# Splitting the key-score weights early: 34 weight tiles split during the second block's attention and kept split in DRAM

## The chip, the cores and the metric

One core of one Trainium2 chip runs the kernel. Times are device microseconds (us) of one execution, from a profile or from timed runs; lower is better. The kernel's own clock starts at its first instruction ("span"); a timed run also holds what lies around the span.

## The reference, cut to what matters

The program is two transformer blocks over 512 tokens of width 1024, float32. Only the second half of the second block matters here: attention with a merge of two branches, and then `peer`, a product-key lookup over a table of 16384 experts.

```python
def peer(h, wq, keys1, keys2, u_tab, v_tab):        # cut
    q = (xc @ wq).reshape(chunk, 8, 2, 128)
    s1, s2 = q[:, :, 0] @ keys1, q[:, :, 1] @ keys2  # 128 scores each, per head
    v1, i1 = top_k(s1, 16); v2, i2 = top_k(s2, 16)
    best, pos = top_k(all 256 sums v1 + v2, 16)      # 16 experts per token and head
    g = softmax(best)
    a = u_tab[eidx] . xc                             # first table
    return (gelu(a) * g) . v_tab[eidx]               # second table
```

## The kernel before, in words

Every float32 product is made of three fp32r products (`mm3`, lines 87 to 89): both operands are split into a high part, `hi`, and a low part, `lo = src - hi`. `split` (lines 66 to 70) makes `hi` with one copy on ACT (L69) and `lo` with one subtraction on DVE (L70), or on POOL where `eng=nc.gpsimd` is given. `wload` (lines 72 to 85) loads a weight tile of 128x1024 floats (512 KB) through the SP queue into one of 4 raw buffers `wraw`, and splits it into one of 3 buffers `whi` and one of 3 buffers `wlo`. These three pools serve the whole kernel.

The order on each engine is made when the kernel is built, by a list scheduler that simulates the program: among the instructions that are ready it takes the one that stands first in the program. In `peer` the order on POOL, and late in it on DVE, is that of the program text. A generator class `Fill` (lines 33 to 44) lets one piece of the program hand out its steps inside the loops of another.

The stages around the change, all in order:

- **Attention of the second block** (`block2`, 8 heads). Each turn of the loop over `h` makes half of a merge tile (`half_merge`: a `w2g` tile and half a `w2b` tile), in every second turn also the next queries (`q_prep`), then the weighted values of head `h` (`values`: transposes, split of the transposed probabilities, products) and the scores of the next head.
- **Merge** (L1370 to L1381): 8 turns over `m`, each with a `w2g` tile, half a `w2b` tile and a few sums.
- **Output projection and norm**: start of `peer`, with 8 `w2o` tiles.
- **Score stage** (`peer`, L1523 to L1602): for each of 8 heads, `scores(h)` loads two tiles of the queries' weights `pwq` (L1529, split with POOL), makes the queries and their 2x128 scores, and finds the top 16 of each on DVE (`top16`, L1388 to L1393); `best16(h)` adds the pairs on POOL (`cand`, L1551), takes the top 16 of the sums and turns them into expert numbers (L1562 to L1593, DVE and ACT). Between them stand `ahead(n)` calls: each runs one `u_chunk`, that is, one of 128 chunks of the first table, `puT[c]`, against all tokens of three tiles, with a gelu on ACT (L1430) and a store to `ad`. Chunks 0 to 27 are made here (4 before the stage's own loop, 2 in each `scores`, 1 in every second `best16`, 4 at the end), and their `lo` is made on POOL. POOL also gathers two table rows per head (L1493) and multiplies them (L1503) for the fourth token tile.
- **Table stages**: one-hot matrices with chunks 28 to 79, then the second table with chunks 80 to 127. Their chunks are split with DVE.

Of the kernel before, what the change touches and what calls it, by code (L numbers as in the profile page):

```python
# [9 lines left out]
F32 = mybir.dt.float32  # L10
F32R = mybir.dt.float32r
# [11 lines left out]
KD = D // 128  # L23
# [5 lines left out]
def f32(ap):  # L29
    return ap.bitcast(F32)  # L30
# [16 lines left out]
class Emit:  # L47
# [1010 lines left out]
            yield from self.filters(pool, psum)  # L1058


    def block2(self, es0):
        self.rstep = RSTEP
        tc, nc, A = self.tc, self.nc, self.A
        mm = nc.tensor.matmul
        tt, ts, stt = nc.vector.tensor_tensor, nc.vector.tensor_scalar, nc.vector.scalar_tensor_tensor
        with ExitStack() as es:
# [162 lines left out]
                            self.split(yhl[:, 0, j], yhl[:, 1, j], y)  # L1229

            pc = es.enter_context(tc.tile_pool(name="b2c", bufs=1))
            ohl = pc.tile([128, 2, 4, S], F32R, name="atT")
            mb = pc.tile([128, KD, S], F32, name="mb")
            with ExitStack() as e2:
# [115 lines left out]
                for h in range(8):  # L1350
                    cur = nxt
                    if h % 2 == 0 and h < 6:
                        nq.append(q_prep(h // 2 + 1))
                    if h < 7:
                        half_merge(1, h + 1, None)
                    values(h, *cur)
                    if h < 7:
                        nxt = scores(h + 1)
# [4 lines left out]
            with ExitStack() as e2:  # L1363
                self.banks(e2, 6)
                m2 = e2.enter_context(tc.tile_pool(name="mg22", bufs=2))
                mh = mg.tile([128, KD, S], F32R, name="mh2")
                ml = mg.tile([128, KD, S], F32R, name="ml2")
                g1 = mg.tile([128, D], F32, name="g1")
                self.dma(g1, self.mod[0:1, 2 * D:3 * D].to_broadcast([128, D]))
                for m in range(KD):  # L1370
                    ps = lin(A["w2g"][2 * m])
                    s = m2.tile([128, S], F32, name="sga")
                    nc.scalar.activation(s, ps, AF.Sigmoid)
                    wh, wl = self.wload(A["w2b"][m, :, 0:512])
                    ps = self.bank()
                    for k in range(4):
                        c = slice(k * 128, k * 128 + 128)
                        self.mm3(ps, wh[:, c], wl[:, c], ohl[:, 0, k], ohl[:, 1, k], k == 0, k == 3)
                    tt(s, ps, s, op=ALU.mult)
                    tt(s, s, mb[:, m], op=ALU.add)  # L1380
                    self.split(mh[:, m], ml[:, m], s)  # L1381
                self.merged = mh, ml, g1, mg


# [10 lines left out]
    def peer(self):  # L1395
# [9 lines left out]
        with ExitStack() as es:  # L1405
# [15 lines left out]
            b = self.mod_cols(pp, self.mod, 3 * D, "pb")  # L1421
            def u_chunk(c, eng=None):

                wh, wl = self.wload(A["puT"][c], eng=eng)
                p = self.acc()
                for k in range(KD):
                    s_ = slice(k * 128, k * 128 + 128)
                    self.mm3(p[:, :TD], wh[:, s_], wl[:, s_], hh[:, k, :TD], hl[:, k, :TD], k == 0, k == KD - 1)
                g = dn.tile([128, TD], F32, name="ga", bufs=4)
                nc.scalar.activation(g, p[:, :TD], AF.Gelu_apprx_tanh)  # L1430
                if c < AHEAD:
                    self.dma(ad[c], g)
                    return None
                return g
# [79 lines left out]
            with ExitStack() as ek:  # L1514
# [7 lines left out]
                def scores(h):  # L1522
                    val = pk.tile([128, NT, 2, 16], F32, name="tkv", bufs=3)  # L1523
                    ixu = pk.tile([128, NT, 2, 16], U32, name="tki", bufs=3)
                    keys = pk.tile([128, 256], F32, name="keys")
                    self.dma(keys, A["pkeys"][h])
                    for half in range(2):
                        wh, wl = self.wload(A["pwq"][2 * h + half], eng=nc.gpsimd if h >= 0 else None)
                        ps = self.acc()  # L1529
                        for k in range(KD):  # L1530
                            c = slice(k * 128, k * 128 + 128)
                            self.mm3(ps, wh[:, c], wl[:, c], hh[:, k], hl[:, k], k == 0, k == KD - 1)
                        q = pk.tile([128, S], F32, name="pq")
                        nc.scalar.activation(q, ps, AF.Copy)
                        p3 = self.bank()
                        for t in range(NT):
                            c = slice(t * 128, t * 128 + 128)
                            mm(p3[:, c], lhsT=q[:, c], rhs=keys[:, half * 128:half * 128 + 128], start=True, stop=True)
                        sk = pk.tile([128, NT, 128], F32, name="sk")
                        nc.scalar.activation(sk, p3.rearrange("p (t n) -> p t n", t=NT), AF.Copy)  # L1540
                        for t in range(NT):
                            self.top16(pk, sk[:, t], 128, val[:, t, half], ixu[:, t, half])
                        ahead(1)
                    return val, ixu
# [215 lines left out]

BLOCKS = ((0, 0, 2, 16), (32, 2, 2, 8), (48, 4, 4, 4), (64, 8, 8, 2))
GLAST = 122
GPOOL = 16
GSHARE = 0.34
OVERFLOW = True
# [172 lines left out]
```

## Time and profile before

| | us |
|---|---|
| median of 3 runs | 2734.28 (2725.38 to 2735.51) |
| the profiled execution, whole | 2726.15 |
| its span | 2724.4 |

One execution was profiled. PE is TensorE's matmuls, PEld its weight loads, DVE VectorE, ACT ScalarE, POOL GpSimd, SP the queue that issues most DMAs. A row of a view by line has: line, engine, operation, tile written <- tiles read, count, then busy time and mean duration, then the idle time of the engine just before and what ended it. "Busy" of an instruction runs from its start to its end, so an instruction that is held up after it started is counted as busy.

### The profile page before, as it was taken

What the parts mean: (1) busy time and instruction counts of PE and PEld (TensorE: products, weight loads), DVE (VectorE), ACT (ScalarE), POOL (GpSimd) and SP (SyncE); (2) the same over time, 40 slices, a digit from 0 to 9 for tenths busy, and PEclk for the clock granted to TensorE, in tenths of its full rate; (3) what the DMA queues carried; (4) which work ended last, traced back from release to release, by engine and by line L of the source; (5) the groups of instructions that cost most, each with busy time, mean ns of one, the idle gap of its engine ahead of it and who ended that gap; (6) DMA issues with size and microseconds to landing.
All of it is one profiled execution on the core that took longest, in us unless ns stands there. A gap on an engine that the chain in (4) does not pass through costs nothing. (4 is left out here: it accounts for less than half of the span.)

```text
span 2724.4 us, 33367 instructions
## 1 busy us (share of the span) xinstructions
PE 2451.1 (90%) x11725; PEld 1919.5 (70%) x11725; DVE 1853.3 (68%) x3133; ACT 1074.9 (39%) x1608; POOL 941.6 (35%) x777
## 2 busy tenths in 40 slices
PE   7999897879977979999798888999899999999997
PEld 5776566423335766668597778989688878988886
DVE  6677965334356576654649999988677767777676
ACT  4554434212215336653433435434433333333333
POOL 1002640101100320000145665430666665666661
PEclk9999998889988988999899889999699999999999
DMA  4115684789975211104543348997589998888884
GB/s 142 62 54 170 224 289 160 283 331 390 400 276 207 93 59 47 39 32 156 172 124 127 126 135 278 344 370 254 203 292 302 304 302 265 306 303 287 293 294 158
DMA packets 215934, 589.47 MB, mean 216 GB/s; under 512 B 30565, under 2 KB 85349, under 8 KB 214740
## 3 DMA queue, kind: packets, MB, share of 16 engines
q1 hardware_dynamic: 170836, 433.91, 45.8%
q0 software_dynamic: 44928, 153.42, 16.3%
q8 instruction: 92, 1.51, 0.2%
q14 instruction: 78, 0.64, 0.1%
HBM read 541.85 MB, written 53.78 MB: 219 GB/s over the span
## 5 line engine op out<-in xcount | busy, mean ns | idle before, releaser
L69 ACT ACTIVATE whi<-wraw 128x1024 fp32r<-128x1024 f32 (+1 forms) x290 | 299.8, 1035 | 489.8 <-PE acc L88 175.0
L87 PE MATMUL acc<-hph,whi 128*128 128x384 f32 (+1 forms) x1152 | 407.1, 354 | 30.1 <-ACT ga L1430 29.2
L89 PE MATMUL acc<-hph,wlo 128*128 128x384 f32 (+1 forms) x1152 | 404.1, 351 | 7.9 <-DVE wlo L70 7.3
L88 PE MATMUL acc<-hpl,whi 128*128 128x384 f32 (+1 forms) x1152 | 402.7, 350 | 0.0
L70 DVE TENSOR_TENSOR wlo<-wraw,whi 128x1024 fp32r<-128x1024 f32 (+1 forms) x242 | 296.8, 1227 | 140.0 <-ACT whi L69 138.0
L70 POOL TENSOR_TENSOR wlo<-wraw,whi 128x1024 fp32r<-128x1024 f32 x48 | 120.1, 2507 | 468.1 <-ACT whi L69 463.4
L87 PEld LDWEIGHTS acc<-hph,whi 128*128 128x128 f32 x1152 | 222.6, 193 | 42.3 <-ACT ga L1430 33.9
L87 PE MATMUL yp<-vhi,wah 128*128 128x512 f32 x732 | 228.4, 392 | 11.3 <-ACT wah L69 11.3
L89 PEld LDWEIGHTS acc<-hph,wlo 128*128 128x128 f32 x1152 | 221.6, 192 | 22.2 <-DVE wlo L70 14.8
L88 PE MATMUL yp<-vlo,wah 128*128 128x512 f32 x732 | 228.3, 391 | 0.0
L1676 POOL TENSOR_TENSOR gw<-gw,ga 128x256 f32<-128x256 f32 x128 | 179.6, 1403 | 141.0 <-DMA ga<-ad 78.0
L88 PEld LDWEIGHTS acc<-hpl,whi 128*128 128x128 f32 x1152 | 222.4, 193 | 7.3 <-DVE hpl L70 0.2
L89 PE MATMUL yp<-vhi,wal 128*128 128x512 f32 x732 | 225.1, 390 | 0.0
L70 DVE TENSOR_TENSOR vlo<-wraw,vhi 128x1024 fp32r<-128x1024 f32 x122 | 156.4, 1282 | 97.0 <-ACT vhi L69 96.9
L1493 POOL DMA_INDIRECT grow<-pu,ei x128 | 148.9, 1164 | 208.0 <-DVE grow L1506 169.5
L1493 POOL DMA_INDIRECT grow<-pvr,ei x128 | 172.6, 1349 | 113.4 <-DVE gy L1510 87.9
L69 ACT ACTIVATE wah<-gw 128x384 fp32r<-128x384 f32 x126 | 66.1, 524 | 276.9 <-POOL gw L1677 217.9
L1510 DVE SCALAR_TENSOR_TENSOR gy<-grow,wt,gy 128x1024 f32<-128x1024 f32 x127 | 164.0, 1291 | 11.5 <-DMA grow<-pvr,ei 9.3
L87 PEld LDWEIGHTS yp<-vhi,wah 128*128 128x128 f32 x732 | 138.0, 189 | 40.8 <-ACT wah L69 14.0
L70 DVE TENSOR_TENSOR wal<-gw,wah 128x384 fp32r<-128x384 f32 x126 | 93.9, 745 | 100.3 <-ACT wah L69 98.4
L89 PEld LDWEIGHTS yp<-vhi,wal 128*128 128x128 f32 x732 | 137.5, 188 | 30.3 <-DVE wal L70 1.8
L88 PEld LDWEIGHTS yp<-vlo,wah 128*128 128x128 f32 x732 | 138.2, 189 | 27.0
(669 smaller groups left out, 5168.8 us busy)
## 6 DMA issues: line engine op xcount, KB each, us to landing
wraw<-wgu SPq DMA_DIRECT2D x128, 512.0 KB
wraw<-puT SPq DMA_DIRECT2D x128, 512.0 KB
wraw<-pv SPq DMA_DIRECT2D x128, 512.0 KB
wraw<-wd SPq DMA_DIRECT2D x64, 512.0 KB
aw<-wada SPq DMA_DIRECT2D x48, 512.0 KB
gd<-gs SPq DMA_DIRECT2D x8, 2048.0 KB
gw<-gd SPq DMA_DIRECT2D x128, 128.0 KB
ad<-ga SPq DMA_DIRECT2D x80, 192.0 KB
```

Source lines behind the costliest of these rows:

```text
L69: nc.scalar.activation(hi, src, AF.Copy)
L70: (eng or nc.vector).tensor_tensor(lo, src, f32(hi), op=ALU.subtract)
L87: mm(ps, lhsT=wh, rhs=xh, start=first, stop=False)
L88: mm(ps, lhsT=wh, rhs=xl, start=False, stop=False)
L89: mm(ps, lhsT=wl, rhs=xh, start=False, stop=last)
L1493: nc.gpsimd.indirect_dma_start(out=r, out_offset=None, in_=A["pu" if i < 128 else "pvr"], in_offset=bass.IndirectOffsetOnAxis(ap=ei[:, s:s ...
L1510: stt(gy, r, wt[:, s:s + 1], gy, op0=ALU.mult, op1=ALU.add)
L1676: nc.gpsimd.tensor_tensor(gw[:, :TG], gw[:, :TG], g[:, :TG], op=ALU.mult)
```

## The change

A generator `presplit` hands out 34 steps: 16 tiles of `pwq` and the first 18 chunks of `puT`. A step loads the tile, splits it (copy on ACT, subtraction on POOL) and stores both halves to DRAM from POOL's queue. Three steps are handed out in each turn of the attention loop (24 in all) and two in each turn of the merge until none is left (the other 10, in five turns). In the score stage the 34 tiles are no longer split: their two halves are loaded straight into a `whi` and a `wlo` buffer.

```diff
+    def presplit(self):
+        tc, nc, A = self.tc, self.nc, self.A
+        self.qd = tc.dram_tile([16, 2, 128, 1024], F32, name="qd")
+        self.ud = tc.dram_tile([NPRE, 2, 128, 1024], F32, name="ud")
+        todo = [(A["puT"][i], self.ud[i]) for i in range(4)] + [(A["pwq"][i], self.qd[i]) for i in range(4)]
+        for i in range(4, max(16, NPRE)):
+            todo += [(A["pwq"][i], self.qd[i])] if i < 16 else []
+            todo += [(A["puT"][i], self.ud[i])] if i < NPRE else []
+        for src, dst in todo:
+            h, l = self.wload(src, eng=nc.gpsimd)
+            self.store(dst[0], f32(h))
+            self.store(dst[1], f32(l))
+            yield
+
+    def presplit_load(self, src):
+        hi = self.whi.tile([128, 1024], F32R, name="whi")
+        lo = self.wlo.tile([128, 1024], F32R, name="wlo")
+        self.dma(f32(hi), src[0])
+        self.dma(f32(lo), src[1])
+        return hi, lo
...
+            fill = Fill(self.presplit())
...
+                    fill(PFILL)
                     values(h, *cur)
...
                     self.split(mh[:, m], ml[:, m], s)
+                    fill(2 if m < KD - 1 else None)
...
-                wh, wl = self.wload(A["puT"][c], eng=eng)
+                wh, wl = self.presplit_load(self.ud[c]) if c < NPRE else self.wload(A["puT"][c], eng=eng)
...
-                        wh, wl = self.wload(A["pwq"][2 * h + half], eng=nc.gpsimd if h >= 0 else None)
+                        wh, wl = self.presplit_load(self.qd[2 * h + half])
...
+NPRE = 18
+PFILL = 3
```

## Rows read from the trace of the kernel before

**Rows 1.** The page's shares of the whole span
```profile
PE 2451.1 (90%) x11725; PEld 1919.5 (70%) x11725; DVE 1853.3 (68%) x3133; ACT 1074.9 (39%) x1608; POOL 941.6 (35%) x777
```

**Rows 2.** Busy time by stretch: attention, merge, projection, score stage
```profile
core 0: us, PE busy (x) PEld busy (x) DVE busy (x) ACT busy (x) POOL busy (x), PEclk, DMA share, GB/s
1050.00:1225.00 175.00, 160.19 (x718) 117.59 (x718) 107.48 (x151) 104.71 (x165) 0.00 (x0) 0.93 0.12 38
1225.00:1292.00 67.00, 66.15 (x289) 53.84 (x288) 33.01 (x44) 25.34 (x35) 0.00 (x0) 1.00 0.47 148
1292.00:1345.00 53.00, 45.38 (x187) 34.08 (x185) 33.42 (x46) 25.63 (x30) 7.83 (x4) 0.94 0.65 215
...
1376.00:1634.00 258.00, 222.30 (x1098) 200.47 (x1098) 220.68 (x904) 101.18 (x159) 151.06 (x100) 0.91 0.41 131
```

**Rows 3.** Lines on POOL and ACT, 1376 to 1634 us
```profile
L70 POOL TENSOR_TENSOR wlo<-wraw,whi 128x1024 fp32r<-128x1024 f32 x40 | 101.0, 2533 | 70.1 <-ACT whi L69 65.4 <-issue 2.9 <-PE acc L89 1.8
L1503 POOL TENSOR_TENSOR grow<-grow,htok 128x1024 f32<-128x1024 f32 x12 | 28.8, 2397 | 0.2
...
L69 ACT ACTIVATE whi<-wraw 128x1024 fp32r<-128x1024 f32 x39 | 41.0, 1052 | 37.1 <-issue 23.5 <-POOL wlo L70 7.8 <-PE acc L88 5.2
```

**Rows 4.** Lines on DVE, same stretch
```profile
L1562 DVE TENSOR_TENSOR gslot<-best 128x64 f32<-128x64 f32 x8 | 26.7, 3341 | 0.0
L1585 DVE TENSOR_TENSOR eq<-pu,i 128x1024 f32<-128x1024 uint32 x14 | 21.0, 1497 | 0.0
...
L1580 DVE TENSOR_SCALAR pu<-pu 128x64 uint32<-128x64 uint32 x7 | 12.3, 1754 | 0.0
L1579 DVE TENSOR_TENSOR pu<-pu,pu 128x64 uint32<-128x64 uint32 x7 | 10.3, 1472 | 0.0
...
L1388 DVE MAX8 best<-cand 128x8 f32<-128x80 f32 x32 | 5.4, 231 | 17.4 <-POOL cand L1551 17.4
...
L1574 DVE TENSOR_SCALAR pu<-pos 128x64 uint32<-128x64 uint32 x7 | 1.2, 170 | 0.0
```

**Rows 5.** Instructions in order of time: the same DVE line held and not held
```profile
1445.85 0.20 DVE L1562 TENSOR_TENSOR gslot<-best 128x64 f32<-128x64 f32 x1
...
1449.93 0.21 DVE L1578 TENSOR_TENSOR pu<-pu,pu 128x64 uint32<-128x64 uint32 x1
...
1505.26 2.39 POOL L1503 TENSOR_TENSOR grow<-grow,htok 128x1024 f32<-128x1024 f32 x1
...
1505.70 4.34 DVE L1562 TENSOR_TENSOR gslot<-best 128x64 f32<-128x64 f32 x1
...
1507.61 2.34 POOL L70 TENSOR_TENSOR wlo<-wraw,whi 128x1024 fp32r<-128x1024 f32 x1
```

**Rows 6.** The same earlier, in the convolution stage: POOL, then two DVE lines
```profile
907.62 2.40 POOL L70 TENSOR_TENSOR wlo<-wraw,whi 128x1024 fp32r<-128x1024 f32 x1 [52.79 <-ACT whi L69]
...
907.77 0.68 DVE L1165 TENSOR_TENSOR y<-bank,kd 128x512 f32<-128x512 f32 x1
...
908.37 2.19 DVE L1160 TENSOR_TENSOR y<-y,y 128x512 f32<-128x512 f32 x1
```

**Rows 7.** PE in order of time: start to start of its products
```profile
1442.10 1.05 PE L1538 MATMUL bank<-keys,pq 128*128 128x128 f32 x8
...
1443.34 0.34 PE L89 MATMUL acc<-hph,wlo 128*128 128x384 f32 x1
...
1446.98 0.34 PE L89 MATMUL acc<-hph,wlo 128*128 128x384 f32 x1
...
1449.71 0.39 PE L89 MATMUL acc<-hph,wlo 128*128 128x512 f32 x1
...
1453.80 0.39 PE L89 MATMUL acc<-hph,wlo 128*128 128x512 f32 x1
```

**Rows 8.** The merge, 1230 to 1292 us: who waited for whom
```profile
ACT whi L69 <- PE acc L88: 18.5, 6, 3.2
```

**Rows 9.** DMA issues from POOL's queue, with time to landing; their instruction
```profile
kf<-fout POOLq DMA_DIRECT2D x8, 512.0 KB, 5.5
...
L59 POOL DMA_DIRECT2D kf<-fout x8: 536/566/583, 685.7 to 808.5; - x8
...
DMA to landing us min/median/max: 2.9/5.5/11.5
```

## The prediction

> **What bounds the kernel now.** I read the shares first: PE is busy 90% of the span and DVE 68% [rows 1], but no share says which stage could give time back. So next the busy time by stretch [rows 2]. In the merge PE is busy for 66.15 of 67 us: nothing can be gained there and anything late is lost. In attention it is 160.19 of 175. In the score stage (1376 to 1634 us, 258 us) PE has 222.30 and DVE 220.68: neither fills it, and each waits for the other.
>
> The lines of that stage show why. POOL makes 40 `lo` halves of 2.533 us, 101.0 us in all, and 28.8 us of row products [rows 3]. DVE's `gslot` subtraction of only 64 columns takes 3.341 us on average [rows 4]; in order of time one takes 0.20 us, another 4.34 us, and the long one spans the end of one POOL product and all of the next POOL split, ending as that ends [rows 5]. The convolution stage shows the same: during a POOL split a DVE instruction that reads one operand from PSUM takes its plain 0.68 us, the next one, with both operands in SBUF, takes 2.19 us [rows 6]. So POOL's work holds up DVE's two-SBUF-operand instructions, and in the score stage these are in the chain that ends each head.
>
> How much? Mean minus plain duration, times count [rows 4, 5]: `gslot` 8 x (3.34 - 0.20) = 25 us; L1580 7 x (1.75 - 0.17, the like L1574) = 11; L1579 7 x (1.47 - 0.21, the like L1578) = 9; L1585 14 x (1.50 - 1.21, the duration that this size of operation shows unheld) = 4. With 17.4 us of idle time before `best`, which waits for POOL's `cand` [rows 4], that is 66 us of DVE's 258.
>
> **The score stage after.** Of the 40 POOL splits 16 are `pwq` and 24 are chunks; chunks 18 to 27, ten of them, stay. So 30 go: 30 x 2.533 = 76 us of POOL's 130 us of splits and products (58%), and 30 x 1.05 = 32 us of ACT copies [rows 3], which lie beside other work. If the hold-ups shrink in proportion, DVE's chain gets back 0.58 x 66 = 38 us.
>
> PE sets the limit. Start to start a 384-column product takes (1446.98 - 1443.34)/21 = 0.173 us, a 512-column one (1453.80 - 1449.71)/18 = 0.227 us, eight key products 1.05 us [rows 7]. The 1098 products are 384 of `pwq`, 128 of keys and 586 of chunks: 87 + 17 + 102 = 206 us at the higher clock; the granted clock of the stage is 0.91 [rows 2]. 258 - 206 = 52 us is all that can go. With PE as busy as in attention (160.19/175 = 0.92), the stage takes 225 us, **33 us less**. That is near the 38 of the DVE account; I take 33, and 15 to 50 as ends.
>
> What is late next there: a tile now comes by two loads of 512 KB instead of one, 30 x 0.52 MB = 16 MB more. Traffic goes from 131 GB/s to (131 x 258 us + 16 MB)/225 us = 220 GB/s; at 131 the engines' share was 0.41 [rows 2], so about 0.7. It fits, but the look-ahead shrinks from 4 raw buffers and 3 split pairs to 3 pairs. SP issues some 30 more DMAs; a chunk's load now waits for a free pair, and behind it on SP wait the `ad` stores and key loads. This I cost at nothing, since two chunks of 4.2 to 5.5 us are still ahead of PE; the third rival below says what it costs if that cover goes.
>
> **Attention.** It gains 24 steps. Each issues a load on SP, a copy of 1.05 us on ACT, a split of 2.40 us on POOL and two stores on POOL of 0.566 us each [rows 3, 6, 9]. ACT goes from 104.71 to 130 us of 175, POOL from nothing to 24 x 3.5 = 85 us [rows 2]. POOL itself is free, so its stores cost nothing there. In its way: ACT copies stand in front of exponentials and of the transposed probabilities; and a POOL split holds DVE's two-operand splits, while the probabilities' `lo` halves read PSUM and pass [rows 6]. PE has 15 us of slack, spread over 7 turns. Ends 0 and +20 us; I take **+5**, nearer to the low end because PE, not ACT or DVE, is the fullest engine by 55 us.
>
> **Merge.** It gains 10 steps in five turns, and here the buffers matter. A turn is 67/8 = 8.4 us of PE, nearly all products: 24 + 12 at 0.227 us = 8.2 us. ACT already waits 18.5 us for PE to free a `whi` buffer [rows 8]. Pair-time of the turn's own two tiles: 8.2 us of products plus their splits, about 3.6 us, from the 1.05 and 1.21 us of a full tile and half of it for a half tile: 11.8. A step keeps a pair from its copy to the landing of its store: 1.05 + 2.40 + 0.57 + 5.5 = 9.5 us [rows 3, 6, 9]. Two steps and the turn's own need (11.8 + 19)/3 = 10.3 us of three pairs, 2.1 more than PE needs; five turns give **+10**. Ends: +2, if the scheduler spreads the steps, and +30 with the longest landing, 11.5 us [rows 9].
>
> The projection after it (45.38 of 53 us on PE, share 0.65 [rows 2]) only sees its loads start later; the first chunks' halves are stored long before. The table stages keep their instructions. Both at 0: what hides a late load there is PE's queue of products; without it the projection loses one landing, about 5 us.
>
> **Sum:** -33 + 5 + 10 = **-18 us**, from 2726.15 for the profiled execution to 2708. That execution stands 8 us (0.3%) below the median of the runs; from the median 2734.28 the same saving gives **2716 us**, 0.66% faster. A measurement of this kernel can tell about 0.5%, 14 us, from no change.
>
> **Rivals.**
>
> *PE at its limit and all steps hidden.* The score stage falls to 208 us (-50), attention costs 0, merge +4: -46, 2688 us. For it: the hold-ups are the chain, and the clock would rise when PE no longer pauses. Against: ACT's queue also makes PE pause, and that is not moved.
>
> *POOL's rest goes on holding DVE.* The change doesn't do what it is shaped for: 29 us of row products and ten splits remain, and one is enough to hold `gslot`, as the product at 1505.26 does [rows 5]. The stage gives 15 us, the steps cost 10: -5, 2729.
>
> *Loads come late.* With three pairs of look-ahead and SP in order, each of 30 tiles makes PE wait 0.7 us: -33 + 21 + 15 = +3, 2737.
>
> *Pairs run out in attention and merge (slower).* With landings of 11.5 us a step keeps a pair for 15.5 us; a merge turn needs (11.8 + 31)/3 = 14.3 us, +6 over PE, in five turns +30; attention, where a turn of 25 us has 75 us of pair-time, loses 10; the score stage gives 20: +20, 2754. It decides once a step keeps a pair for over (3 x 8.2 - 11.8)/2 = 6.4 us in the merge; below that nothing is lost.
>
> *The hold-up only moves (slower).* Each of 34 POOL splits holds one DVE split by 2.19 - 0.68 = 1.5 us [rows 6], in stages where PE waits for those splits: +51 instead of +15: -33 + 51 = +18, 2752. For it: in the merge four DVE instructions of each turn have both operands in SBUF. Against: in attention the fullest DVE lines read PSUM. The Trainium skill states this as a rule, in "SBUF — State Buffer", section "Who interferes with whom": a VectorE instruction with two SBUF inputs and a GpSimd instruction that reads SBUF exclude each other, and whichever issues first keeps the other out to its end. That speaks against moving POOL work under DVE splits; the trace agrees (4.34 us against 0.20), and by the rule alone this rival would be the forecast.
>
> **Chances.** Forecast 0.36, PE at its limit 0.16: faster 0.52. POOL's rest 0.14, late loads 0.13: within 0.5% 0.27. Pairs 0.12, moved hold-up 0.09: slower 0.21. The range 2686 to 2752 takes in every case as priced but the last part of the pairs' case, and leaves out about 2 in 10, for the ends of the first and of the slower cases. Faster alone would be 2686 to 2720.
>
> **What would show it.** In the profile after: about 10 POOL splits left in the score stage; `gslot` near 0.2 us while chunks below 18 run and long again in the last three heads; the stage near 225 us with PE above 0.9 of it. In attention, POOL at some 85 us, PE idle up by 5. In the merge, PE idle up by about 2 us in each of five turns, waiting for weights whose pair a store still holds. Wrong, if the score stage stays above 245 us (then loads or POOL's rest decide: SP's or PE's waits tell which), or if attention and merge together grow by over 30 us.

## The result and the profile after

The changed kernel takes **2770.95 us** (median of 4 runs, 2770.07 to 2771.94) against 2733.80 for the kernel before on the same chip: ratio 1.0142, 95% interval 1.0121 to 1.0163. It is 1.4% slower, where 2716 us had been forecast, and above the range's end of 2752. In the table a stage is measured between landmarks that both kernels have (attention: first to last exponential; merge: to the last gated sum; projection: to the first query tile; score stage: to the first one-hot matrix), read from the two profiled executions, in us.

| stage | before | after | difference |
|---|---|---|---|
| up to attention | 1041.0 | 1040.7 | -0.3 |
| attention | 163.9 | 196.6 | +32.7 |
| merge | 83.6 | 125.3 | +41.7 |
| projection and norm | 97.1 | 89.4 | -7.7 |
| score stage | 273.4 | 241.2 | -32.2 |
| one-hot stage | 289.7 | 288.4 | -1.3 |
| the rest | 767.3 | 778.7 | +11.4 |

The rest is code that the change doesn't touch. The profiled execution of before is the odd one there: the runs below have 770.5 to 779.3, so those 11 us are not the change's. What has to be explained is +74 in attention and merge against -40 behind them.

The page's shares of after, which answer to [rows 1], show as little as they did before the change: PE 89% for 90%.

```profile
PE 2469.3 (89%) x11725; PEld 1929.2 (70%) x11725; DVE 1845.8 (67%) x3133; ACT 1074.9 (39%) x1608; POOL 975.0 (35%) x845
```

Busy time by stretch of after, which answers to [rows 2]: attention, merge, score stage.

```profile
core 0: us, PE busy (x) PEld busy (x) DVE busy (x) ACT busy (x) POOL busy (x), PEclk, DMA share, GB/s
1041.00:1237.00 196.00, 165.77 (x647) 119.89 (x646) 108.72 (x140) 122.88 (x181) 68.73 (x59) 0.83 0.53 186
1237.00:1362.00 125.00, 96.73 (x375) 73.12 (x374) 55.10 (x59) 47.18 (x64) 44.91 (x40) 0.87 0.73 260
...
1452.00:1693.00 241.00, 221.50 (x1169) 203.76 (x1167) 214.06 (x927) 91.17 (x170) 91.56 (x76) 0.97 0.64 215
```

The same view of before, with the first, second and last stretch between the same landmarks.

```profile
1041.00:1205.00 164.00, 150.70 (x662) 109.45 (x662) 104.89 (x143) 105.13 (x163) 0.00 (x0) 0.94 0.12 37
1205.00:1288.00 83.00, 79.62 (x360) 64.17 (x359) 40.07 (x55) 32.84 (x48) 0.00 (x0) 0.98 0.36 118
...
1386.00:1659.00 273.00, 233.00 (x1162) 211.83 (x1160) 242.70 (x929) 114.59 (x196) 157.91 (x103) 0.91 0.43 139
```

Read PE's busy time against the stretch. In attention PE's idle time went from 13.3 to 30.2 us and its busy time from 150.7 to 165.8 for the same products; in the merge idle from 3.4 to 28.3, busy from 79.6 to 96.7. So about 42 us of the loss are pauses, and 32 us are the same products run at a lower granted clock (0.94 to 0.83, 0.98 to 0.87). (Both profiles count 1022 products in the two stages together, but 15 of them moved from attention's stretch to the merge's; so the sums hold, and the split between the two stages is rough.)

The score stage did what was forecast. Its lines on POOL and DVE, 1443 to 1666 us, answer to [rows 3, 4]; L1589 is the `gslot` line, L1607 and L1606 are the L1580 and L1579 of before.

```profile
L70 POOL TENSOR_TENSOR wlo<-wraw,whi 128x1024 fp32r<-128x1024 f32 x10 | 26.2, 2626 | 33.0 <-ACT whi L69 30.5 <-PE acc L89 2.5
...
L1589 DVE TENSOR_TENSOR gslot<-best 128x64 f32<-128x64 f32 x7 | 7.7, 1102 | 0.0
...
L1606 DVE TENSOR_TENSOR pu<-pu,pu 128x64 uint32<-128x64 uint32 x7 | 3.7, 527 | 0.0
...
L1607 DVE TENSOR_SCALAR pu<-pu 128x64 uint32<-128x64 uint32 x7 | 3.5, 500 | 0.0
```

Ten POOL splits are left, `gslot` takes 1.10 us on average where it took 3.34, the two others 0.5 where they took 1.5 and 1.75, and PE is busy for 92% of the stage. All eight `gslot` instructions (shortest, median and longest in ns):

```profile
L1589 DVE TENSOR_TENSOR gslot<-best x8: 207/240/4457, 1477.3 to 1666.9; 128x64 f32<-128x64 f32 x8
```

One by one they take 0.21 to 0.25 us in the first five heads, where POOL splits nothing, and 2.13, 4.46 and 2.68 us in the last three, where the ten splits are left. That is the sign which the prediction had named, head by head.

Now the waits of after. First PE's in attention (1041 to 1237 us), then ACT's, DVE's and PE's in the merge (1237 to 1362); each row: who <- whom, total, times, longest, in us.

```profile
PE acc L1355 <- ACT sg L1282: 10.4, 7, 2.9
PE bank L87 <- ACT hn_y L197: 6.5, 2, 3.3
PE z L1340 <- ACT pr L1344: 5.4, 3, 1.8
...
ACT whi L69 <- PE acc L88: 34.0, 8, 7.2
ACT mh L69 <- DVE sga L1406: 17.3, 7, 4.3
...
DVE wlo L70 <- PE acc L89: 26.9, 4, 7.5
...
PE acc L89 <- DVE wlo L70: 16.9, 5, 4.7
```

The two lines of before (1041 to 1205 us) that answer to PE's first and third:

```profile
PE acc L1330 <- ACT sg L1257: 1.6, 4, 0.5
...
PE z L1315 <- ACT pr L1319: 1.3, 2, 1.0
```

In attention PE waits for ACT's *own* attention work, the gate `sg`, the norm `hn_y`, the exponentials `pr`: ACT comes to them late, though it is busy for only 122.88 of 196 us. What ACT's weight copies wait for in attention, after:

```profile
ACT whi L69 <- PE acc L88: 19.4, 7, 4.0
ACT whi L69 <- PE bank L88: 12.9, 5, 5.8
...
ACT whi L69 <- DMA qd<-whi: 3.1, 3, 1.4
```

Together with 3.2 us that have no releaser these are 38.6 us, where before had 9.3. Most of it is waiting for PE to be done with one of the three shared `whi` buffers; only 3.1 us wait for a step's store to land.

In the merge weights wait for a buffer, PE for weights, and ACT for a sum that DVE makes (`sga`).

Why ACT is late shows in order of time: POOL and ACT in attention; then, from 1294, POOL, DVE and ACT in the merge.

```profile
1105.35 2.39 POOL L70 TENSOR_TENSOR wlo<-wraw,whi 128x1024 fp32r<-128x1024 f32 x1 [21.55 <-ACT whi L69]
...
1104.20 1.06 ACT L69 ACTIVATE whi<-wraw 128x1024 fp32r<-128x1024 f32 x1 [3.33 <-PE acc L88]
...
1112.38 1.06 ACT L69 ACTIVATE whi<-wraw 128x1024 fp32r<-128x1024 f32 x1 [1.42 <-DMA qd<-whi]
1113.35 0.88 ACT L1344 ACTIVATE pr<-z,mx 128x768 f32<-128x768 f32 x1
...
1115.63 0.69 ACT L197 ACTIVATE hn_y<-bank,eps 128x512 f32<-128x512 f32 x1
...
1294.26 4.67 POOL L70 TENSOR_TENSOR wlo<-wraw,whi 128x1024 fp32r<-128x1024 f32 x2
...
1295.36 4.13 DVE L1406 TENSOR_TENSOR sga<-sga,mb 128x512 f32<-128x512 f32 x1
...
1299.52 0.63 ACT L69 ACTIVATE mh<-sga 128x512 fp32r<-128x512 f32 x1 [4.13 <-DVE sga L1406]
```

And a store in the chain that ended last:

```profile
1107.69 4.62 DMA qd<-whi
```

A step's copy (1104.20) fills a `whi` buffer, POOL subtracts, its store leaves at 1107.69 and lands at 1112.31. ACT's copy at 1112.38 waits for that landing: ACT is idle for 1.42 us before it, and an exponential and a norm stand behind it. Landings of stores take 10.9 us of that chain in attention. In the merge two POOL splits run back to back from 1294.26 to 1298.93; DVE's sum of two SBUF tiles, 0.69 us in the merge of before, starts at 1295.36 and ends at 1299.49, and ACT's split of that sum waits 4.13 us.

### The profile page after: what moved, and what is told of

The parts are those of the page before. It is cut to its first block, busy times and chain, and to the rows that moved or that the text cites. A ratio compares the mean times of both kernels' runs of the same rounds, so it can differ in the third digit from the quotient of the medians.

```text
span 2769.0 us, 33706 instructions
## 1 busy us (share of the span) xinstructions
PE 2469.3 (89%) x11725; PEld 1929.2 (70%) x11725; DVE 1845.8 (67%) x3133; ACT 1074.9 (39%) x1608; POOL 975.0 (35%) x845
## 4 chain that ended last, share of the span: by engine, by line
PE 47%; DMA 17%; DVE 15%; issue 11%; ACT 6%; POOL 3%; SPq 0%; DVEq 0%; ACTq 0%; POOLq 0%
PE acc L87 6%; PE acc L89 6%; PE acc L88 6%; DMA wraw<-puT 5%; PE bank L658 4%; PE yp L88 3%; PE yp L87 3%; PE yp L89 3%; DVE wlo L70 3%; PE bank L87 2%; PE bank L89 2%; PE bank L88 2%; DMA grow<-pvr,ei 2%; DMA aw<-wada 2%; DVE gy L1537 2%
## 5 line engine op out<-in xcount | busy, mean ns | idle before, releaser
L87 PE MATMUL acc<-hph,whi 128*128 128x384 f32 (+1 forms) x1152 | 400.6, 348 | 18.7 <-ACT ga L1457 17.6
```

The lines of the kernel that those rows point to most:

```text
L87: mm(ps, lhsT=wh, rhs=xh, start=first, stop=False)
```

## The experiments

Theory A (ours): **queue heads**. A step's copy or subtraction that waits for a transfer, a buffer or another engine stands at the head of its engine's queue and holds up the stage's own instructions behind it (e13 below has such a wait of 126.8 us). Theory B: **POOL holds DVE**, as in [rows 5, 6]. Theory C: **traffic**; 34 x 2 stores of 512 KB in attention and merge, where the DMA engines' share went from 0.12 to 0.53 and from 0.36 to 0.73. Theory D, later: **too many steps**, wherever they stand.

All results first: the ratio to the kernel before on the same chip, and stages of the profiled execution, in us.

| run | median | ratio [95%] | attention | merge | projection | score |
|---|---|---|---|---|---|---|
| before | | | 163.9 | 83.6 | 97.1 | 273.4 |
| after | 2770.95 | 1.0142 [1.0121, 1.0163] | 196.6 | 125.3 | 89.4 | 241.2 |
| e1 | 2701.10 | 0.9896 [0.9867, 0.9925] | 168.6 | 82.7 | 90.7 | 241.1 |
| e2 | 2814.64 | 1.0312 [1.0282, 1.0342] | 196.0 | 126.1 | 97.3 | 271.5 |
| e3 | 2761.51 | 1.0117 [1.0088, 1.0146] | 184.9 | 90.3 | 97.2 | 274.6 |
| e4 | 2739.08 | 1.0026 [1.0012, 1.0039] | 181.7 | 103.4 | 91.6 | 241.3 |
| e5 | 2807.96 | 1.0274 [1.0244, 1.0304] | 184.2 | 91.9 | 98.3 | 274.4 |
| e6 | 2747.75 | 1.0052 [1.0032, 1.0071] | 176.0 | 84.6 | 95.8 | 274.4 |
| e7 | 2745.67 | 1.0057 [1.0042, 1.0073] | 190.7 | 101.8 | 92.5 | 238.8 |
| e8 | 2740.24 | 1.0033 [1.0019, 1.0048] | 206.1 | 83.2 | 90.1 | 241.5 |
| e9 | 2784.18 | 1.0193 [1.0152, 1.0235] | 178.6 | 120.2 | 97.7 | 274.6 |
| e10 | 2746.14 | 1.0047 [1.0022, 1.0073] | 197.8 | 89.6 | 90.9 | 241.3 |
| e11 | 2728.95 | 0.9995 [0.9983, 1.0007] | 163.9 | 83.6 | 97.4 | 274.7 |
| e12 | 2733.96 | 1.0014 [1.0002, 1.0026] | 172.8 | 105.9 | 89.7 | 244.4 |
| e13 | 2732.39 | 1.0017 [1.0001, 1.0033] | 165.6 | 82.7 | 119.0 | 247.8 |
| e14 | 2715.86 | 0.9952 [0.9939, 0.9966] | 167.3 | 84.0 | 95.8 | 250.1 |
| e15 | 2730.56 | 1.0000 [0.9981, 1.0019] | 183.7 | 84.4 | 95.8 | 247.4 |
| e16 | 2708.82 | 0.9922 [0.9897, 0.9946] | 171.6 | 83.8 | 90.3 | 250.0 |

A profiled execution's first exponential stands between 1038.8 and 1048.9 us (in e5 at 1090.8), so totals also differ by up to 10 us in what lies ahead of these stages. In e10, e12, e13 and e14 the first steps are made there, from about 1005 us on; what they cost there is not told apart.

All diffs are against the changed kernel.

### Gain and cost apart

**e1**, the score stage's part alone: one step, whose tile all 34 loads read. It leaves out the other 33 tiles.

```diff
-                    fill(PFILL)
+                    if h == 0:
+                        fill(1)
...
-                    fill(2 if m < KD - 1 else None)
...
-                wh, wl = self.presplit_load(self.ud[c]) if c < NPRE else self.wload(A["puT"][c], eng=eng)
+                wh, wl = self.presplit_load(self.ud[0]) if c < NPRE else self.wload(A["puT"][c], eng=eng)
...
-                        wh, wl = self.presplit_load(self.qd[2 * h + half])
+                        wh, wl = self.presplit_load(self.ud[0])
```

> Only one of the 34 steps is left, in the first turn of the attention, and all 34 loads of the score stage read the two halves of that one tile; so the queries' weights and chunks 1 to 17 are left out of the computation. All theories agree on what is left: the stage from the first pq copy to the last, 217 us before and 182 us in the changed kernel, stays near 182, attention and merge go back to what they were, and the time is 2734 - 35 = about 2699 us (2688 to 2712). If it is over 2720, the score stage's gain depends on what else the steps moved.

Measured: 31 us faster than before (2731.97 in these runs). The gain is real and of the forecast's size.

**e2**, the steps alone: all 34 made and stored, the score stage as before.

```diff
-                wh, wl = self.presplit_load(self.ud[c]) if c < NPRE else self.wload(A["puT"][c], eng=eng)
+                wh, wl = self.wload(A["puT"][c], eng=eng)
...
-                        wh, wl = self.presplit_load(self.qd[2 * h + half])
+                        wh, wl = self.wload(A["pwq"][2 * h + half], eng=nc.gpsimd)
```

> All 34 steps run in attention and merge, and the score stage loads and splits its tiles itself as before, so nothing of the computation is left out. If the loss lies in the steps alone: 2771 + 35 = about 2806 us (2795 to 2820), attention +32 and merge +42 us as in the changed kernel. Under 2780 would mean that the loss comes from loading the halves, not from making them.

Measured: 83 us slower, with the attention and merge of after. So what these two stages lose comes from making the steps, not from loading the halves. The two parts do not quite add up: -31 and +83 are +52, and the whole change has +37. In the profiles 8 of these 15 us lie ahead of attention (e2's first exponential is at 1048.9 us, after's at 1040.7) and 5 in e1's attention (168.6 for 163.9); why is open. (These lines are in e3, e5, e6, e9 and e11 too, where they are not shown again.)

### Stores, or what holds up the queues

**e3** is e2 without the stores.

```diff
-            self.store(dst[0], f32(h))
-            self.store(dst[1], f32(l))
```

> As the run with the steps alone, but no step stores its halves. Pairs theory (a step keeps a hi and a lo buffer of the shared three until its stores land, some 5.5 us longer than the split): a step's hold falls from about 9.5 to 3.5 us, the merge needs less than PE does again, and attention and merge lose under 25 us together instead of 74: 2760 us or less. Hold-up theory (POOL's splits hold DVE's instructions with two SBUF operands): the same 34 splits hold the same instructions, 2790 us or more, with L1406 still near 4 us in the merge.

Measured: 53 of the 83 us go with the stores. By stage these are 36 us of the merge, which is nearly as before, 11 of attention, which keeps 21, and 8 ahead of both. It doesn't tell traffic from waiting: without a store there is neither.

**e11** tells them apart: the stages of before, and 68 stores of 512 KB in the same places, from three small buffers that nothing else uses. POOL fills one as soon as a small tile of that turn is there.

```diff
-            h, l = self.wload(src, eng=nc.gpsimd)
-            self.store(dst[0], f32(h))
-            self.store(dst[1], f32(l))
+            o = self.own.tile([128, 512], F32, name="own")
+            nc.gpsimd.memset(o, 0.0)
+            nc.gpsimd.tensor_copy(o[:, 0:1], self.gate)
+            for d in dst[0], dst[1]:
+                self.store(d.rearrange("p (a b) -> p a b", a=2), o[:, None, :].to_broadcast([128, 2, 512]))
```

> The kernel before with 68 stores of 512 KB added in the places of the steps' stores: no load, no split; each pair of stores reads a small tile of its own that POOL clears and marks from the same turn's result, so the stores come turn by turn. What lands in the two DRAM arrays is not used. Traffic theory (the stores slow the loads or POOL's queue): attention and merge +25 us or more, 2756 us or more. Queue-head theory (a step's copy on ACT or subtraction on DVE stands at the head of its queue and waits for a step's load or store, with attention's own instructions behind it; with low halves on DVE these waits sum up to 43 us, without stores to 0.2): no ACT or DVE instruction waits here, 2731 to 2742 us.

Busy time by stretch of e11, attention and merge:

```profile
1043.00:1207.00 164.00, 150.72 (x661) 109.40 (x662) 104.96 (x143) 105.19 (x163) 39.97 (x72) 0.94 0.41 153
1207.00:1290.00 83.00, 79.66 (x359) 64.16 (x358) 40.00 (x55) 32.79 (x48) 33.07 (x61) 0.98 0.86 320
```

At 320 GB/s and a share of 0.86 in the merge, PE has the busy time and the clock that it has in before. Theory C is refuted up to this share: stores cost nothing there by their traffic. The Trainium skill says the same in "SBUF — State Buffer", section "Who interferes with whom": a DMA never contends with a compute engine. e11 agrees, for stores of SBUF tiles.

**e5** was to tell the same in another way: e2, with stores that read a tile which no step writes.

```diff
-            self.store(dst[0], f32(h))
-            self.store(dst[1], f32(l))
+            self.store(dst[0], self.other)
+            self.store(dst[1], self.other)
...
+            self.other = f32(hh[:, 0:2]).rearrange("p k s -> p (k s)")
```

> As the run with the steps alone (2815 us), with the same 68 stores of 512 KB from POOL's queue, but they read a tile that nothing writes in these stages, so that a hi or lo buffer is free as soon as it is split; what lands in the two DRAM arrays is left out. Pairs theory: as without stores, about 2762 us (2755 to 2780). If the stores cost by their traffic or by POOL's time at the queue, it stays at 2800 to 2815.

Inconclusive by its time: with nothing to wait for, all 68 stores came ahead of attention, whose first exponential was 50 us later (1090.8 for 1041.0). From 840 to 945 us the DMA engines' share was 1.02 at 403 GB/s, and POOL stood for 59 us until earlier stores of its own had landed. Which of the two cost the 50 us is not shown, so traffic at a full share is not cleared. Attention and merge, 184.2 and 91.9, are then those of the steps without stores.

**e9** keeps the stores among the steps: e2, but POOL copies half of each `lo` to a buffer of its own, and both stores read that.

```diff
-            self.store(dst[0], f32(h))
-            self.store(dst[1], f32(l))
+            o = self.own.tile([128, 512], F32, name="own")
+            nc.gpsimd.tensor_copy(o, f32(l[:, :512]))
+            for d in dst[0], dst[1]:
+                self.store(d.rearrange("p (a b) -> p a b", a=2), o[:, None, :].to_broadcast([128, 2, 512]))
```

> The steps alone, low halves on POOL, and 68 stores of 512 KB in their places in time; but each step first copies half of its low part into a tile of its own (one more POOL operation of some 0.7 us) and the stores read that tile, so that the shared hi and lo buffers are free after the split; what lands in the two DRAM arrays is left out. The run whose stores read an old tile could not tell, because its stores all ran ahead of the attention (its first exponential began 50 us later). Pairs theory: attention and merge together lose about 30 us, as without stores: 2762 to 2775 us. Traffic theory (the stores slow the loads, or POOL): 2795 us or more.

Measured: 2784 us, between the two expectations. Attention is 17 us shorter than in e2, the merge only 6. POOL's work is longer here (61.05 us in the merge for 44.97 in e2), and the merge's sum still takes 1.58 us on average; that POOL's work stands in for the stores is the likely reason, not a shown one.

### POOL holding DVE

**e4**: the low halves on DVE, so that POOL only issues stores.

```diff
-            h, l = self.wload(src, eng=nc.gpsimd)
+            h, l = self.wload(src)
```

> The changed kernel, with the steps' low halves made on DVE (about 1.22 us each, 41 us in all) and not on POOL. Hold-up theory: no POOL operation is left to hold DVE, and the merge falls from 100 us by 20 us or more, attention by 10: 2740 us or less. Pairs theory: a step's hold shrinks by only 1.2 us, and DVE has 41 us more to do: 2760 to 2780 us.

Measured: 32 us less than after. The merge's sum takes 0.69 us again, so theory B holds for a part. But attention and merge are still 38 us longer than before. The waits of e4 (1045 to 1335 us):

```profile
ACT whi L69 <- DMA qd<-whi: 8.6, 3, 4.4
ACT whi L69 <- DMA ud<-whi: 8.4, 5, 3.0
...
DVE wlo L70 <- DMA ud<-wlo: 11.4, 7, 2.7
DVE wlo L70 <- DMA qd<-wlo: 9.5, 7, 2.7
```

Both engines now stand before a store's landing, 38 us in all.

**e6** is e2 with both cures, low halves on DVE and no stores.

```diff
-            h, l = self.wload(src, eng=nc.gpsimd)
-            self.store(dst[0], f32(h))
-            self.store(dst[1], f32(l))
+            h, l = self.wload(src)
```

> The steps alone, with the low halves on DVE and without stores: neither of the two suspected costs is left, only 34 loads, 34 copies on ACT (36 us) and 34 subtractions on DVE (41 us). If the two explain the loss and add up: 2815 - 53 - 32 = 2730 us, at or below the kernel before within 10 us. If they are the same loss seen twice: about 2755 to 2762, as without stores alone.

Half a miss: the waits on stores are gone and the merge is as before, but attention keeps 12 us. The two causes overlap (53 for the stores; 45 for POOL's subtractions, as e2's 83 less what e4 has over e1, 38; but 67 for both together), and 12 us are left for 34 copies and 34 subtractions in ACT's and DVE's queues by themselves.

**e8**: e4 with all steps in attention.

```diff
-PFILL = 3
+PFILL = 5
```

> The whole change with the low halves on DVE and five steps handed out in each turn of the attention, none in the merge. Pairs theory: a turn of attention has 75 us of buffer time and needs 16 + 5 x 8.3 = 58, the merge has none of it: attention +25, merge 0, score stage -32: about 2727 us (2718 to 2740). If it is the steps' count that costs wherever they stand, it stays at 2739 or more.

The same time as e4: the merge is cured, attention takes on what the merge had. The cost goes with the steps.

**e7**: e4, storing only the low half; the score stage loads the raw tile and copies the high half on ACT.

```diff
-            self.store(dst[0], f32(h))
...
-        self.dma(f32(hi), src[0])
+        w = self.wraw.tile([128, 1024], F32, name="wraw")
+        self.dma(w, raw)
+        self.nc.scalar.activation(hi, w, AF.Copy)
```

> The whole change with the low halves on DVE, but only the low half is stored; the score stage loads the raw tile, copies it to hi on ACT as before, and loads the low half. Pairs theory: the hi buffer is free after the subtraction, and half the stores are gone, so attention and merge lose some 20 us instead of 38 of the run with DVE (2739), while the score stage gives a few us less than 32 for its 34 copies: 2715 to 2730 us. If the hi copies on ACT were what held the score stage, it gives only 15 and the time is 2735 or more.

A miss. Half the stores bring nothing. DVE still stands 17.1 us until low halves have landed (20.9 in e4). ACT's 17.0 us of e4 are gone, but attention is 9 us longer than in e4, and why is not shown.

**e10**: e4 with high and low buffers of the steps' own, two of each, half as wide.

```diff
-            h, l = self.wload(src, eng=nc.gpsimd)
-            self.store(dst[0], f32(h))
-            self.store(dst[1], f32(l))
+            w = self.wraw.tile([128, 1024], F32, name="wraw")
+            self.dma(w, src)
+            for n in range(2):
+                c = slice(n * 512, n * 512 + 512)
+                h = self.ownh.tile([128, 512], F32R, name="ownh")
+                l = self.ownl.tile([128, 512], F32R, name="ownl")
+                self.split(h, l, w[:, c])
+                self.store(dst[0][:, c], f32(h))
+                self.store(dst[1][:, c], f32(l))
```

> The whole change with low halves on DVE, and each step made in two halves of 512 columns in four small buffers of its own (two hi, two lo), so that no step takes a shared hi or lo buffer. Both theories' costs are gone; left are the loads, the copies and subtractions (16 us when the steps ran alone with neither cost) and the stores' traffic. Pairs and hold-up theories together: 2731 - 31 + 16 = 2716 us (2706 to 2728), faster than both kernels. Traffic theory: 2735 us or more.

A miss that corrected the theory: 2746 where 2716 was expected. The high and low buffers are no longer shared, and DVE still stands before them (1045 to 1335 us):

```profile
DVE ownl L70 <- DMA qd<-ownl: 10.0, 7, 3.9
...
DVE ownl L70 <- DMA ud<-ownl: 5.3, 5, 2.0
```

(To make room for such buffers, some temporaries of attention have 512 columns in place of 516, here and in e12, e13, e14 and e16; what that does by itself was not tried.) ACT stands for 8.5 us more in the same way, and for 17.3 us until a step's raw tile has landed. Against e4 the merge is 14 us shorter and attention 16 us longer. So buffers of the steps' own are no cure as long as what waits for a step stands on ACT's and DVE's queues.

### The steps on an engine with nothing else to do

POOL has no instruction of its own in attention and merge [rows 2]. So a step that waits there should hold up nobody in these two stages.

**e12**: as e10, but copy and subtraction on POOL too, and 24 steps, all in attention.

```diff
-                self.split(h, l, w[:, c])
+                nc.gpsimd.tensor_copy(h, w[:, c])
+                nc.gpsimd.tensor_tensor(l, w[:, c], f32(h), op=ALU.subtract)
...
-NPRE = 18
+NPRE = 8
```

(the first two lines against e10)

> 24 steps only (the queries' weights and 8 chunks), all in the attention, each made wholly on POOL: copy and subtraction in halves of 512 columns, in four small buffers of its own, so that neither ACT nor DVE ever waits for a step. The score stage keeps 10 more splits, so it should give some 22 of its 32 us. Queue-head theory: left is what POOL's work holds up on DVE, about +12 us in attention and 0 in the merge: 2721 us (2712 to 2730), faster than both kernels. Traffic theory: attention +27 or more, 2736 us or more.

Attention +9 as expected, where e10 had +34. The steps' half tiles made within attention are 32 here and 43 in e10, in the same kind of buffers; so a half tile costs attention 0.3 us on POOL and 0.8 us on ACT and DVE.

But the merge +22. Its waits (1041 to 1340 us), ACT's and SP's; then the load that ACT waits longest for, and last the same load in before:

```profile
ACT whi L69 <- DMA wraw<-w2g: 19.2, 3, 11.6
...
SPq L55 <- PE po L1369: 24.0, 1, 24.0
...
1240.84 0.50 SPq L55 DMA_DIRECT2D wraw<-w2g  x1
...
1208.08 0.33 SPq L55 DMA_DIRECT2D wraw<-w2g  x1
```

The merge's own weights come late. In before this `w2g` load leaves ahead of the load of `x_tok` (1225.62), which waits for PE. Here it stands behind it (1235.12, after those 24.0 us), and behind five loads of the steps' raw tiles that left from 1201 us on. POOL ran behind and made its last steps up to 1254 us. That the waiting steps' raw tiles held the buffers, and so moved this load back, is likely but not shown. The queue is another one, the pattern the same.

**e14**: e12 with 16 steps (the queries' weights), two in a turn.

```diff
-NPRE = 18
-PFILL = 3
+NPRE = 0
+PFILL = 2
```

> As the run with everything on POOL, but 16 steps in place of 24, raw tiles still from the buffers that the block shares. If the merge's 22 us came from a backlog of steps on POOL that kept raw buffers past attention's end: no backlog with 16, merge 84 to 88 us, total about 2718. If the shared raw buffers cost the merge even without a backlog (rival): merge 95 us or more, attention longer too, total 2728 or more.

Busy time by stretch of e14, attention, merge and score stage:

```profile
1047.00:1214.00 167.00, 151.50 (x660) 109.79 (x659) 109.62 (x143) 104.84 (x161) 72.76 (x99) 0.93 0.47 156
1214.00:1298.00 84.00, 80.71 (x363) 64.91 (x362) 40.47 (x55) 33.38 (x50) 0.00 (x0) 0.98 0.37 116
...
1394.00:1644.00 250.00, 223.25 (x1166) 204.00 (x1164) 218.22 (x927) 101.83 (x183) 121.22 (x89) 0.95 0.53 180
```

Attention +3, merge +0.4, score stage -23: 0.5% faster than before. In attention and merge no wait of ACT or DVE on a DMA for a weight tile is left.

**e13**: 16 steps, nothing shared: POOL loads quarter tiles into raw buffers of its own.

```diff
+            for n in range(4):
+                c = slice(n * 256, n * 256 + 256)
+                w = self.ownr.tile([128, 256], F32, name="ownr")
+                self.store(w, src[:, c])
...
+                nc.gpsimd.tensor_copy(h, w)
+                nc.gpsimd.tensor_tensor(l, w, f32(h), op=ALU.subtract)
...
-NPRE = 18
-PFILL = 3
+NPRE = 0
+PFILL = 2
```

> 16 steps (the query weights alone) of four quarter tiles each, copies, subtractions, stores and raw loads all on POOL's queue, with raw, high and low buffers that nothing else uses; ACT, DVE and SP issue nothing for the steps. If the loss is in-order queues whose head waits for a step's transfer or buffer (ours): attention +5 to +10 us (POOL holds DVE a little), merge as before (84 us), score stage some 20 us shorter, total 2716 to 2720. If any splitting on POOL beside attention costs as it did in the run with everything on POOL (rival): merge 95 to 106 us and total 2730 or more.

Attention and merge are those of before (165.6 and 82.7), though POOL is busy for 142 us of attention; so splitting on POOL, in quarter tiles, costs them next to nothing. But the projection is 22 us longer, and a part of the expectation fell. In order of time on POOL:

```profile
1209.32 0.62 POOL L1078 CAST ownh<-ownr 128x256 fp32r<-128x256 f32 x1 [0.43 <-DMA ownr<-pwq]
1336.75 2.38 POOL L70 TENSOR_TENSOR wlo<-wraw,whi 128x1024 fp32r<-128x1024 f32 x1 [126.81 <-ACT whi L69]
1339.10 1.17 POOL L1079 TENSOR_TENSOR ownl<-ownr,ownh 128x256 fp32r<-128x256 f32 x1
...
1356.04 0.56 POOL L59 DMA_DIRECT2D qd<-ownl  x1
```

Who waited, 1290 to 1415 us, on PE and on ACT:

```profile
PE bank L853 <- ACT xn L847: 32.7, 3, 29.9
...
ACT sqj L863 <- DMA qd<-ownl: 19.0, 1, 19.0
```

The last quarters of the last tile came behind a subtraction of one of the score stage's first tiles (1336.75), which stood at POOL's head for 126.8 us until ACT had made its high half. Their last store landed at 1358.11, and two of the norm's instructions had waited for that landing: ACT's first sum of squares for 19.0 us, and on SP the load of one of the norm's inputs for 10.1. (Why these two depend on it is not shown; that their tiles lie where the steps' buffers lay is likely.) It is queue-head waiting a third time: one instruction stood for 126.8 us, and PE was idle for 29.9.

**e15** asks whether e14 is fast because its steps are few (theory D): 16 steps, placed as the change places them.

```diff
-NPRE = 18
-PFILL = 3
+NPRE = 0
+PFILL = 2
```

> The change as it is, with 16 steps (the query weights alone, two in a turn of attention, none in the merge): copies on ACT, low halves on POOL, the shared buffers. If the place of the steps decides (ours: a step's copy at ACT's head, in shared buffers that a store has to free): attention +15 to +30 us although only two steps come in a turn, ACT and DVE wait for DMAs, total 2725 or more. If the number of steps alone decides (rival): attention +3 to +8 and merge +0 as with 16 steps on POOL, total 2714 to 2720.

Attention +20 where the same 16 steps on POOL cost +3, and 15 us in the medians: at the same number the place decides. The number counts too: in this place 16 steps cost attention and merge 21 us, 34 steps 74. (e14 also has buffers of its own; that these alone are no cure, e10 shows.) PE's waits in its attention (1041 to 1225 us):

```profile
PE acc L1355 <- ACT sg L1282: 6.3, 5, 2.2
PE z L1340 <- ACT pr L1344: 4.0, 2, 2.7
```

PE waits for ACT again, 10.3 us in these two rows for 2.2 in the same of e14. One part of the expectation fell: ACT waits 0.8 us for a DMA here, and DVE 4.1 us. What stands in front of ACT's own work are the copies themselves (ACT is busy for 118.5 us of attention, 105.2 in e14) and their waits for other things than a DMA (weight copies stand for 20.3 us in all, 9.2 in e14). The clock falls with the pauses, to 0.86, and PE's busy time is 9 us longer than in e14.

**e16**: e14 with 20 steps, four chunks more.

```diff
-NPRE = 18
-PFILL = 3
+NPRE = 4
+PFILL = 2
...
-                    fill(PFILL)
+                    fill(3 if h % 2 else 2)
```

> As the run with 16 steps on POOL, with 20 (four chunks of the first table more; two and three steps in alternate turns of attention). If POOL keeps up: score stage some 3 us shorter than with 16, attention and merge the same, total about 2713. If 20 already leave a backlog that keeps raw buffers into the merge: merge 90 us or more, total 2718 or more.

The fastest complete kernel here, 2708.82 us, 0.78% under before. Its profiled execution was the slowest of its seven (2719.15); in it PE pauses in attention for 13.3 us, as before, and the clock alone (0.87) makes the stage longer. The median of 2709 is the expected 2713 or a little better; which stage gave it, that execution doesn't show.

## Why the prediction was wrong, point by point

- **Score stage, -33: right.** -32.2 in the profile, -31 alone (e1). PE's limit held: 92% busy as assumed. The hold-ups did not shrink in proportion: they went where the splits went and stayed where they stayed. In 1452 to 1693 us the clock rose to 0.97, which "PE at its limit" had named; but the stage did not go to -50.
- **Loads in two parts at nothing: right.** In the score stage traffic is 215 GB/s at a share of 0.64 (forecast 220 and 0.7), and "loads come late" did not happen: PE waits there for no DMA.
- **Projection and table stages at 0: nearly.** The projection is 7.7 us shorter, also in e1; the first chunks no longer need their splits there.
- **Attention, +5: the first step that failed**; +32.7. It was taken "nearer to the low end because PE, not ACT or DVE, is the fullest engine by 55 us". (These 55 us were read against ACT before the change; with the 130 us that the text itself gives ACT they are 30.) A sum of busy times says how much fits into a stage, not what stands in front of what. The ACT copies that the text named as being "in its way" were priced as 1.05 us of work, without the wait that each may carry (ACT stands 38.6 us before weight copies, for 9.3), the instructions behind it, and PE's lower clock, about 15 of the 32.7 us. The stores, put at nothing there because POOL is free, are 11 of the 32.7 (e3).
- **Merge, +10: the second**; +41.7. The pair-time count was sound in kind: the one hold that was followed, in attention, took 8.1 us (1104.20 to 1112.31), over the 6.4 from which the rival decides. But it counted only buffers against PE. In the merge of after ACT waits 34.0 us for them, for 18.5 in [rows 8], DVE 26.9; it left out that POOL ran behind, so that 13 of its subtractions fell into the merge, not 10, and held the sums on which each turn ends; e4, with the subtractions on DVE, takes 22 us off the merge. The lower clock is about 17 of the 41.7 us, and no term stood for it.
- **The rivals.** "Pairs run out" and "the hold-up only moves" were both slower and both happened; each was priced as if it came alone (40 and 51 us for the two stages; together 74), with 0.21 for both. L1406 takes 4.13 us beside two POOL splits. The low halves on DVE gain 32 us with stores (e4) and 14 without (e3 against e6), each time less what the subtractions cost DVE; with them 38 us of the 74 are left. The rule of the Trainium skill in "SBUF — State Buffer", section "Who interferes with whom", by which the second of these would have been the forecast, had the sign right. About half of the loss remains when POOL subtracts nothing (e4), so that half is of another kind.
- **The test named in advance** ("wrong if attention and merge together grow by over 30 us") gave the right answer: 74.

Shown: the gain (e1), that the cost is the steps' (e2), that traffic up to a share of 0.86 costs nothing (e11), POOL's hold (e4), that for the same steps the engine decides (e10 against e12, e14 against e15), that buffers of one's own are no cure on a busy queue (e10). Only argued: how attention's 33 us divide into work in front, waits for a shared buffer and PE's clock. The stores are 11 (e3); the causes overlap, and e6 and e15 give 12 and 20 us for steps with next to no waits for stores.

## What to carry to other kernels

Work that is moved into a stage costs by the queue it stands on, not by the engine's free time: ask of each moved instruction what it waits for, and what stands behind it on the same engine. Put such work, with all its waits, on an engine that has nothing of its own in that stage, with no more of it than that engine finishes there; and look for the last shared thing (a buffer, a load queue, the next stage's instruction on that engine). Where PE is the bound, a pause can cost more than its length: here 42 us of pauses came with 32 us of lower clock.

## What was not expected of the hardware

- Stores and loads at 320 GB/s, a share of 0.86, beside a PE busy for 79.66 of 83 us cost nothing measurable (e11: ratio 0.9983 to 1.0007).
- In e13 the clock stayed down after a pause. Busy time by stretch, in and after the pause in its projection:

```profile
1350.00:1370.00 20.00, 1.72 (x7) 1.08 (x7) 3.87 (x16) 8.47 (x13) 2.16 (x4) 0.50 0.46 180
1370.00:1390.00 20.00, 12.48 (x37) 8.36 (x37) 14.62 (x31) 5.75 (x8) 0.00 (x0) 0.51 0.00 0
1390.00:1412.00 22.00, 21.71 (x119) 20.25 (x119) 3.75 (x8) 7.68 (x11) 5.22 (x5) 1.00 0.57 192
```

  PE is busy for 1.72 of 20 us, and the granted clock is 0.50, the lower level of 1.2 GHz; in the next 20 us PE is busy for 12.48 at the same level, and only the third stretch is back at 2.4 GHz.
- The clock's part in the loss: with pauses that grew by 42 us in attention and merge, the same products took 32 us longer. In e16's profiled attention the idle time is that of before (13.3 us) and the clock still lower (0.87 for 0.94), with PE busy for 158.3 us in place of 150.6: pauses in total don't settle it, and where they lie was not tried.
